# A depthwise convolution on three engines: ScalarE and GpSimd take the shared sum, VectorE keeps its running sum in PSUM

## The chip, the core and the metric

One core of a Trainium2 chip runs the whole kernel as one program. The metric is the time of an execution in device microseconds; each kernel is run several times and the median counts. Five engines matter here: TensorE (matmuls), VectorE, ScalarE and GpSimd (arithmetic on tiles of 128 partitions), and SyncE, which issues the transfers. On-chip data lie in SBUF, the results of matmuls in the eight banks of PSUM, each 128 x 512 float32.

## The reference

The reference is a small decoder trunk on 1024 tokens with 1024 features: layer 0 mixes tokens by a convolution, layer 1 by an attention with forget gates; each layer then attends to 256 memory tokens and runs a feed-forward network. Only the convolution is touched:

```python
def conformer_conv(h, w_pw1, b_pw1, w_dw, b_dw, ln_g, ln_b, w_pw2, b_pw2):
    u = h @ w_pw1 + b_pw1
    a, gate = jnp.split(u, 2, axis=-1)
    u = a * jax.nn.sigmoid(gate)
    u = lax.conv_general_dilated(          # depthwise: 31 taps, causal, each feature by itself
        u, w_dw[:, None, :], window_strides=(1,), padding=[(30, 0)],
        feature_group_count=D_MODEL) + b_dw
    u = jax.nn.silu(layernorm(u, ln_g, ln_b))
    return u @ w_pw2 + b_pw2
```

## The kernel before, in words

Features lie on the partitions, in eight chunks of 128 (called channels below, m = 0 to 7), tokens along the free dimension. `conv_layer` (L293) goes over the channels in this way:

- `gated_unit` (L362) runs for each half of the tokens. Two groups of 24 matmuls (8 chunks of the input, 3 passes each for float32 accuracy) make the gate and the value. Each group fills one PSUM bank of a pool of two (`pm`). ScalarE turns the gate into a sigmoid `sg` (L368); VectorE adds the bias to the value, multiplies by `sg` and writes `u` (L370). This copy frees the value's bank. `u` holds even and odd tokens apart, with 15 zeros ahead of each for the padding, which GpSimd sets (L301).
- `convolve` (L386) makes 512 even and 512 odd output tokens from `u`. Two neighbouring taps are treated together: the sum of both weights times the odd input is the same for even and odd outputs. This shared sum is `both`: one product with bias (L396) and 15 products added in a chain (L400). Then each half adds its own taps on the differences `d0` and `d1` of neighbouring inputs (L393, L394): 16 steps for the first half, 15 for the second (L408), each a multiplication by a per-partition weight and an addition. All of this is VectorE's. The two halves sum into their own tiles of `X`.
- After each channel VectorE adds the new `X` to `acc` of its half (L354), which is the sum that the layer norm needs.
- `memory_matrices` (L433), a generator that is advanced a step at a time from `conv_layer`, prepares matrices for the attention to the memory tokens: for each of 2 layers and 4 heads, 32 matmuls with `mem`, 16 with `kt` and 8 with `vt`. They use a PSUM pool of their own (`pps`, four banks), and ScalarE moves most of their results out (L468, L483, L501). They do not depend on the convolution and can stand between its matmuls.
- When all channels are done, `layer_norm` (L306) runs for each half (mean, L314; variance, L183; scaling, L317; SiLU on ScalarE, L318; split into high and low parts, L148), and the second linear layer (`linear`, with `add_x`, L321) follows with 16 groups of 24 matmuls.

The order of the work on each engine is fixed when the program is built: a scheduler places the instructions by their priority in the program and by its own estimate of when each could start, and each engine then runs its own list in that order. An instruction that waits holds up everything behind it on its engine. Scratch tiles called "t" in the pool `nrm` rotate through four buffers; an instruction that writes the next one waits until the last reader of that buffer is done.

The weights of a channel are split into a high part by ScalarE (`wh`, L151) and a low part by VectorE (`wl`, L148).

Of the kernel before, what the change touches and what calls it, by code (L numbers as in the profile page):

```python
# [12 lines left out]
F32 = mybir.dt.float32  # L13
F32R = mybir.dt.float32r
AF = mybir.ActivationFunctionType
ALU = mybir.AluOpType
# [3 lines left out]
P = 128  # L20
# [3 lines left out]
HALF = 512  # L24
# [12 lines left out]
HALVES = (slice(0, HALF), slice(HALF, S))  # L37
# [49 lines left out]
def trunk(ctx, tc, a, out):  # L87
    nc = tc.nc
    act, dve, pool, pe = nc.scalar, nc.vector, nc.gpsimd, nc.tensor
# [14 lines left out]
    def col(name, i):  # L104
        return par[:, COLS[name] + i : COLS[name] + i + 1]
# [22 lines left out]
    def open_x():  # L128
        xp = xpool.enter_context(tc.tile_pool(name="x", bufs=1, side="right", reuse_waits="tile"))
        return Halves(xp)  # L130

    def load_x(x, src, sl):
        for c in range(NCH):
            nc.sync.dma_start(x[:, c, sl], src[:, c, sl])

    X = open_x()
    nrm = ctx.enter_context(tc.tile_pool(name="nrm", bufs=2))
# [3 lines left out]
    def bank(p):  # L141
        return p.tile([P, HALF], F32, name="mm", tag="mm")

    def banks(n):
        return tc.tile_pool(name="pm", bufs=n, space=PSUM, reuse_waits="tile")
# [144 lines left out]
        dve.tensor_tensor(X[:, m, sl], t, X[:, m, sl], op=ALU.add)  # L290


    def conv_layer(pm, prep):  # L293
        with tc.tile_pool(name="conv", bufs=2) as cp:
            for sl in HALVES:
                next(prep)
                load_x(X, a["xT"], sl)
            def padded():

                u = cp.tile([P, 2, (PAD + S) // 2], F32, name="u")  # L300
                pool.memset(u[:, :, : PAD // 2], 0.0)  # L301
                return u

            pairs = tap_sums(cp)

            def layer_norm(s, acc):  # L306

                nm = nrm.tile([P, 4], F32, name="nm")
                with tc.high_priority(offset=SMALL_FIRST):
                    dve.tensor_scalar(nm, token_mean(acc), -1.0, None, op0=ALU.mult)  # L310
                nmb = spread(nm)
                C = [X[:, m, HALVES[s]] for m in range(NCH)]
                for c in C:
                    dve.tensor_tensor(c, c, nmb, op=ALU.add)  # L314
                rb = spread(inverse_rms(C, LN_EPS))
                for m, c in enumerate(C):
                    dve.tensor_tensor(c, c, rb, op=ALU.mult)  # L317
                    act.activation(c, c, AF.Silu, bias=col("ln_b", m), scale=col("ln_g", m))  # L318
                    split(*(y.rearrange("p (n s) -> p s n", s=2)[:, s, :] for y in ss[m]), c)

            def add_x(m, sl, t):  # L321
                x = nrm.tile([P, HALF], F32, name="x", tag="t", bufs=4)
                nc.sync.dma_start(x, a["xT"][:, m, sl])
                dve.scalar_tensor_tensor(
                    X[:, m, sl], t, col("pw2_b", m), x, op0=ALU.add, op1=ALU.add
                )

            def gate_weights(m):
                return [weights(a["pw1"][2 * m + j]) for j in (1, 0)]

            hs = operands()
            ahead = gate_weights(0)
            u = padded()
            for sl in HALVES:
                normalize(hs, "mix0", sl)
                next(prep)
                gated_unit(pm, cp, 0, ahead, hs, u[:, :, PAD // 2 :], sl)
            acc = [cp.tile([P, HALF], F32, name=f"acc{s}", bufs=1) for s in range(2)]
            for m in range(NCH):
                if m:  # L340
                    u = padded()
                    for sl in HALVES:
                        gated_unit(pm, cp, m, ahead, hs, u[:, :, PAD // 2 :], sl)
                if m + 1 < NCH:
                    ahead = gate_weights(m + 1)
                for _ in range(2):
                    next(prep, None)

                convolve(cp, m, u, pairs[:, m])
                for s, sl in enumerate(HALVES):  # L350
                    if m == 0:
                        act.copy(acc[s], X[:, m, sl])
                    else:
                        dve.tensor_tensor(acc[s], acc[s], X[:, m, sl], op=ALU.add)  # L354
            ss = operands()
            for s in range(2):
                layer_norm(s, acc[s])
            for _ in prep:
                pass
            linear(pm, lambda m: weights(a["pw2"][m]), NCH, ss, add_x)  # L360
# [15 lines left out]
    def tap_sums(cp):  # L376

        n = TAPS // 2
        w = par[:, COLS["dw_w"] : COLS["dw_w"] + NCH * TAPS].rearrange("p (m t) -> p m t", m=NCH)
        sums = cp.tile([P, NCH, n + 1], F32, name="sums", bufs=1)  # L380
        dve.tensor_copy(sums[:, :, n : n + 1], w[:, :, 2 * n :])
        two = w[:, :, : 2 * n].rearrange("p m (t s) -> p m t s", s=2)
        dve.tensor_tensor(sums[:, :, :n], two[:, :, :, 0], two[:, :, :, 1], op=ALU.add)
        return sums

    def convolve(cp, m, u, sums):  # L386


        n, k = S // 2, TAPS // 2
        even, odd = u[:, 0, :], u[:, 1, :]  # L390
        d0 = cp.tile([P, n + k], F32, name="d0")
        d1 = cp.tile([P, n + k - 1], F32, name="d1")
        dve.tensor_tensor(d0, even[:, : n + k], odd[:, : n + k], op=ALU.subtract)  # L393
        dve.tensor_tensor(d1, even[:, 1 : n + k], odd[:, : n + k - 1], op=ALU.subtract)  # L394
        both = cp.tile([P, n], F32, name="both")
        dve.tensor_scalar(  # L396
            both, odd[:, :n], sums[:, 0:1], col("dw_b", m), op0=ALU.mult, op1=ALU.add
        )
        for j in range(1, k + 1):
            dve.scalar_tensor_tensor(  # L400
                both, odd[:, j : j + n], sums[:, j : j + 1], both, op0=ALU.mult, op1=ALU.add
            )
        out = [X[:, m, sl] for sl in HALVES]
        for s, d, taps in ((0, d0, k + 1), (1, d1, k)):
            y = both
            for j in range(taps):
                w = col("dw_w", m * TAPS + 2 * j + s)
                dve.scalar_tensor_tensor(  # L408
                    out[s], d[:, j : j + n], w, y, op0=ALU.mult, op1=ALU.add
                )  # L410
                y = out[s]

# [13 lines left out]
    @contextmanager  # L428
    def prep_pools(n):
        with tc.tile_pool(name="prep", bufs=2) as pp, tc.tile_pool(name="pps", bufs=n, space=PSUM) as pq:  # L430
            yield pp, pq
# [928 lines left out]
            od[head // 2, i * HD : (i + 1) * HD, (b - 1) * P : (b + 1) * P], ol  # L1360
        )

    with prep_pools(4) as pools, banks(2) as pm:
        conv_layer(pm, chain(*(memory_matrices(*pools, l) for l in range(2))))
    sums = mem_attention(0)
    xd = dram.tile([P, NCH, S], F32, name="xd")
    first_normalized, first_weights = [], []
# [3 lines left out]
    for sl in HALVES:  # L1371
        rb = firsts if sl.start == 0 else spread(rms_of_sums(seconds, RMS_EPS))
        for c in range(NCH):
            y = X[:, c, sl]
# [71 lines left out]
```

## Time and profile before

| | |
|---|---|
| median of 3 runs | 2822.2 us (2816.68 to 2823.24) |
| profiled execution | 2825.31 us |
| its span | 2823.3 us |
| TensorE's mean granted clock in it | 0.991 |
| first write of `both` | 79.1 us |
| last step of L408 starts | 387.0 us |

Busy time is the time in which an engine had an instruction at work. Matmuls are pipelined and their ends are modelled, so two neighbouring rows of TensorE overlap in part; how often they start is read from the difference of two start times. A row of the timeline gives start, duration, engine, line and operation, with a count where equal neighbours are merged; in brackets stands how long the engine sat idle before it and who released it. A row of a group gives the count, then the summed busy time and the mean of one in nanoseconds, then idle time. The chain of waits is followed back from the last instruction and shows at each moment what the end of the program waited for.

### The profile page before, as it was taken

The numbers are of one execution on the slowest core, as the hardware profiler recorded it, in microseconds if no ns is written. First come the engines' busy times: TensorE is split into PE (matmuls) and PEld (weight loads), VectorE is DVE, ScalarE is ACT, GpSimd is POOL, SyncE is SP. The second block draws the span as 40 slices with busy tenths as digits, with TensorE's granted clock in tenths as the row PEclk, the third lists the DMA queues.
The fourth block names the chain that finished last, engine by engine and source line by source line (L and its number), as shares of the span: only waits on it lengthen the run. The fifth ranks groups of instructions, "written<-read, shape, count | busy, mean of one in ns | idle before, by whom it ended". The sixth has DMA issues, their size and how long they took to land.

```text
span 2823.3 us, 36214 instructions
## 1 busy us (share of the span) xinstructions
PE 2740.8 (97%) x12968; PEld 2261.3 (80%) x12968; DVE 2030.9 (72%) x3358; ACT 1278.3 (45%) x2293; POOL 703.1 (25%) x473
## 2 busy tenths in 40 slices
PE   8999999999999999999899999989999999989998
PEld 6777777888888877888688888878888788878886
DVE  5999984555776576777788888875546855577776
ACT  5212143433555553333466666673423655543332
POOL 0000000000065625774000000000000365525773
PEclk9999999999999999999899999999999999999999
DMA  6334364322165585652222221243213455655651
GB/s 219 120 119 135 114 206 124 101 90 70 65 230 177 178 309 187 227 199 89 69 68 70 57 65 55 69 136 98 94 64 105 149 176 190 218 208 197 227 201 61
DMA packets 165428, 390.68 MB, mean 138 GB/s; under 512 B 17264, under 2 KB 46192, under 8 KB 164992
## 3 DMA queue, kind: packets, MB, share of 16 engines
q1 hardware_dynamic: 165248, 388.37, 40.9%
q8 instruction: 102, 1.67, 0.2%
q14 instruction: 78, 0.64, 0.1%
HBM read 270.79 MB, written 113.31 MB: 136 GB/s over the span
## 4 chain that ended last, share of the span: by engine, by line
PE 74%; DVE 12%; ACT 5%; DMA 5%; issue 3%; POOL 1%; SPq 0%; DVEq 0%; POOLq 0%; ACTq 0%
PE mm L1070 34%; PE mm L269 29%; PE mm L1255 5%; DVE w L148 2%; DVE op L148 2%; DVE x L408 1%; PE mm L1341 1%; DVE x L1310 1%; DMA ua<-x 1%; ACT x L1315 1%; PE mm L1353 1%; PE mm L1354 1%; DVE both L400 1%; DVE wl L148 1%; ACT pth L151 1%
## 5 line engine op out<-in xcount | busy, mean ns | idle before, releaser
L1070 PE MATMUL mm<-op,w 128*128 128x512 f32 x5424 | 1242.4, 391 | 24.5 <-ACT m L955 8.7
L1070 PEld LDWEIGHTS mm<-op,w 128*128 128x128 f32 x5424 | 1020.5, 189 | 243.2 <-ACT m L955 9.6
L269 PE MATMUL mm<-op,wh 128*128 128x512 f32 x1056 | 330.5, 394 | 4.2 <-DVE op L148 4.2
L148 DVE TENSOR_TENSOR w<-r,w 128x512 fp32r<-128x512 f32 x264 | 262.6, 998 | 30.5 <-ACT w L653 30.5
L653 ACT CAST w<-r 128x512 fp32r<-128x512 f32 x264 | 163.3, 622 | 262.0 <-PE mm L1070 233.2
L269 PEld LDWEIGHTS mm<-op,wh 128*128 128x128 f32 x1056 | 200.2, 190 | 48.5 <-DVE op L148 6.5
L1255 PE MATMUL mm<-op,wh 128*128 128x512 f32 x736 | 231.4, 396 | 0.0
L148 DVE TENSOR_TENSOR w<-t,w 128x512 fp32r<-128x512 f32 x180 | 178.2, 1005 | 63.2 <-ACT w L653 63.1
L269 PE MATMUL mm<-op,wl 128*128 128x512 f32 x528 | 210.5, 400 | 7.1 <-DVE wl L148 6.2
L207 POOL TENSOR_TENSOR r<-v,mhalf 128x4 f32<-128x4 f32 (+1 forms) x15 | 16.8, 1117 | 741.0 <-DVE v L205 741.0
L647 POOL TENSOR_TENSOR t<-r,t 128x512 f32<-128x512 f32 x104 | 174.9, 1681 | 91.4 <-DVE w L148 54.2
L653 ACT CAST w<-t 128x512 fp32r<-128x512 f32 x180 | 112.0, 622 | 169.8 <-PE mm L1070 140.6
L151 ACT CAST wh<-raw 128x1024 fp32r<-128x1024 f32 x96 | 100.7, 1050 | 193.8 <-PE mm L269 97.5
L865 POOL TENSOR_TENSOR x<-x,x 128x512 f32<-128x512 f32 x112 | 160.2, 1455 | 112.6 <-ACT x L878 101.6
L967 DVE TENSOR_TENSOR x<-mm,x 128x512 f32<-128x512 f32 x160 | 109.5, 684 | 91.1 <-PE mm L1070 73.7
L1255 PEld LDWEIGHTS mm<-op,wh 128*128 128x128 f32 x736 | 139.2, 189 | 26.7
L269 PE MATMUL mm<-op,xsh 128*128 128x512 f32 x512 | 158.0, 393 | 0.0
L1255 PE MATMUL mm<-op,wl 128*128 128x512 f32 x368 | 155.0, 421 | 1.9 <-ACT q L1275 1.9
L151 ACT CAST pth<-mm 128x512 fp32r<-128x512 f32 (+1 forms) x224 | 105.9, 495 | 108.5 <-PE mm L556 80.8
L408 DVE SCALAR_TENSOR_TENSOR x<-d,par,x 128x512 f32<-128x512 f32 x232 | 154.5, 746 | 0.0
L647 POOL TENSOR_TENSOR t<-r,r 128x512 f32<-128x512 f32 x52 | 80.2, 1542 | 295.1 <-DMA r<-in_ff_w 191.0
L1315 ACT ACTIVATE x<-x,nb 128x128 f32<-128x128 f32 (+7 forms) x128 | 99.5, 778 | 109.3 <-DVE nb L1313 100.0
(188 smaller groups left out, 4689.6 us busy)
## 6 DMA issues: line engine op xcount, KB each, us to landing
r<-in_ff_w SPq DMA_DIRECT2D x128, 512.0 KB, 4.0
op<-ua SPq DMA_DIRECT2D x80, 512.0 KB, 6.8
us<-x SPq DMA_DIRECT2D x128, 256.0 KB, 2.9
op<-us SPq DMA_DIRECT2D x64, 512.0 KB, 5.6
raw<-mvo SPq DMA_DIRECT2D x32, 512.0 KB, 3.4
ua<-ul SPq DMA_DIRECT2D x64, 256.0 KB, 2.2
ua<-uh SPq DMA_DIRECT2D x60, 256.0 KB, 2.3
raw<-in_pw SPq DMA_DIRECT2D x24, 512.0 KB, 4.7
```

Of the source, the lines that this page charges most:

```text
L148: dve.tensor_tensor(lo, src, hi.bitcast(F32), op=ALU.subtract)
L151: act.copy(hi, src)
L269: pe.matmul(out_ps, x, y, start=i == 0, stop=i == len(terms) - 1)
L400: dve.scalar_tensor_tensor(both, odd[:, j : j + n], sums[:, j : j + 1], both, op0=ALU.mult, op1=ALU.add)
L408: dve.scalar_tensor_tensor(out[s], d[:, j : j + n], w, y, op0=ALU.mult, op1=ALU.add)
L647: (dve if g in (2, 3, UP, UP + 1) else pool).tensor_tensor(t, raws[g, x], raws[g, y], op=ALU.subtract)
L653: act.copy(highs[n][0], raws[steps[n][:2]])
L865: eng.tensor_tensor(u[g, x], y1, y2, op=op_)
L967: dve.tensor_tensor(v, sums[key], v, op=ALU.add)
L1070: pe.matmul(sums[key], y, z, start=first and i == 0, stop=n == last_of[key] and i == len(terms) - 1, skip_group_check=True,)
L1255: pe.matmul(t, x, y, start=n == 0, stop=n == len(terms) - 1)
L1315: act.activation(x[:, :n], x[:, :n], AF.Exp, bias=nb, accum_out=rs)
```

## The change

- The product with bias that starts `both` becomes a ScalarE activation. Each of the 15 further products becomes a ScalarE activation with a scale, written to a scratch tile `tap` (one of the four "t" buffers), and a GpSimd addition `both = both + tap`.
- The steps on `d0` and `d1` stay on VectorE, but the running sum is kept in a PSUM bank `acc` of a new pool with one bank; only the last step of each half writes `X`. Both halves use the same bank, so the second half's chain follows the first's.
- The pool for the memory matrices' products shrinks from four banks to three, which makes room for the new bank.
- `d0` and `d1` have one buffer each instead of two.

```diff
-    def convolve(cp, m, u, sums):
+    def convolve(cp, pc, m, u, sums):
         n, k = S // 2, TAPS // 2
         even, odd = u[:, 0, :], u[:, 1, :]
-        d0 = cp.tile([P, n + k], F32, name="d0")
-        d1 = cp.tile([P, n + k - 1], F32, name="d1")
+        both = cp.tile([P, n], F32, name="both")
+        act.activation(both, odd[:, :n], AF.Identity, scale=sums[:, 0:1], bias=col("dw_b", m))
+        for j in range(1, k + 1):
+            t = nrm.tile([P, HALF], F32, name="tap", tag="t", bufs=4)
+            act.activation(t, odd[:, j : j + n], AF.Copy, scale=sums[:, j : j + 1])
+            pool.tensor_tensor(both, both, t, op=ALU.add)
+        d0 = cp.tile([P, n + k], F32, name="d0", bufs=1)
+        d1 = cp.tile([P, n + k - 1], F32, name="d1", bufs=1)
         dve.tensor_tensor(d0, even[:, : n + k], odd[:, : n + k], op=ALU.subtract)
         dve.tensor_tensor(d1, even[:, 1 : n + k], odd[:, : n + k - 1], op=ALU.subtract)
-        both = cp.tile([P, n], F32, name="both")
-        dve.tensor_scalar(
-            both, odd[:, :n], sums[:, 0:1], col("dw_b", m), op0=ALU.mult, op1=ALU.add
-        )
-        for j in range(1, k + 1):
-            dve.scalar_tensor_tensor(
-                both, odd[:, j : j + n], sums[:, j : j + 1], both, op0=ALU.mult, op1=ALU.add
-            )
-        out = [X[:, m, sl] for sl in HALVES]
+        acc = bank(pc)
         for s, d, taps in ((0, d0, k + 1), (1, d1, k)):
             y = both
             for j in range(taps):
+                o = X[:, m, HALVES[s]] if j == taps - 1 else acc
                 w = col("dw_w", m * TAPS + 2 * j + s)
-                dve.scalar_tensor_tensor(
-                    out[s], d[:, j : j + n], w, y, op0=ALU.mult, op1=ALU.add
-                )
-                y = out[s]
+                dve.scalar_tensor_tensor(o, d[:, j : j + n], w, y, op0=ALU.mult, op1=ALU.add)
+                y = acc
...
-    with prep_pools(4) as pools, banks(2) as pm:
-        conv_layer(pm, chain(*(memory_matrices(*pools, l) for l in range(2))))
+    with prep_pools(3) as pools, banks(2) as pm, banks(1) as pc:
+        conv_layer(pm, pc, chain(*(memory_matrices(*pools, l) for l in range(2))))
```

The scheduler's order changes with it. VectorE before, at channel 1 (`x_79` and `x_80` are the tiles of `X` of its two halves, `d_866` and `d_867` its differences):

```order
L393 TENSOR_TENSOR d_866<-u 128x527
L394 TENSOR_TENSOR d_867<-u 128x526
L396 TENSOR_SCALAR both<-u,sums,par 128x512
L400 SCALAR_TENSOR_TENSOR both<-u,sums,both 128x512 x15
L408 SCALAR_TENSOR_TENSOR x_79<-d_866,par,both 128x512
L408 SCALAR_TENSOR_TENSOR x_80<-d_867,par,both 128x512
L408 SCALAR_TENSOR_TENSOR x_79<-d_866,par,x_79 128x512
```

VectorE now, at the same channel (`mm` on the left of L409 is the new bank; the `u` of L370 is channel 2's):

```order
L402 TENSOR_TENSOR d_948<-u 128x526
L409 SCALAR_TENSOR_TENSOR mm<-d_947,par,both 128x512
L409 SCALAR_TENSOR_TENSOR mm<-d_947,par,mm 128x512 x11
L370 SCALAR_TENSOR_TENSOR u<-mm,par,sg 128x2x256
L409 SCALAR_TENSOR_TENSOR mm<-d_947,par,mm 128x512 x3
L409 SCALAR_TENSOR_TENSOR x_79<-d_947,par,mm 128x512
L409 SCALAR_TENSOR_TENSOR mm<-d_948,par,both 128x512
L354 TENSOR_TENSOR acc_567<-acc_567,x_79 128x512
```

The two halves' chains no longer alternate, and the copy of the next channel's `u` stands behind steps that need `both`.

ScalarE before, from channel 2's sigmoids to channel 3's (`vt` is a memory product):

```order
L368 ACTIVATE sg<-mm,par 128x512 x2
L151 CAST wh<-raw 128x1024 x2
L468 COPY vt<-mm 128x512
L368 ACTIVATE sg<-mm,par 128x512 x2
L151 CAST wh<-raw 128x1024
```

ScalarE now, at the same place:

```order
L368 ACTIVATE sg<-mm,par 128x512 x2
L151 CAST wh<-raw 128x1024 x2
L394 ACTIVATE both<-u,par,sums 128x512
L397 ACTIVATE tap<-u,sums 128x512 x15
L467 COPY vt<-mm 128x512
L368 ACTIVATE sg<-mm,par 128x512 x2
L151 CAST wh<-raw 128x1024 x2
```

The taps stand ahead of the next channel's sigmoids.

TensorE before, in the second linear layer after the layer norm (`op` with `wh` and `wl` are its matmuls, `praw,vt` memory products):

```order
L269 MATMUL mm<-op,wl 128x512 x2
L269 MATMUL mm<-op,wh 128x512 x3
L269 MATMUL mm<-praw,vt 128x512 x4
L269 MATMUL mm<-op,wh 128x512
L269 MATMUL mm<-op,wl 128x512
```

TensorE now, at the same place:

```order
L269 MATMUL mm<-op,wl 128x512 x2
L269 MATMUL mm<-op,wh 128x512 x2
L269 MATMUL mm<-praw,vt 128x512 x4
L269 MATMUL mm<-mem,praw 128x256 x32
L269 MATMUL mm<-kt,praw 128x256 x12
L269 MATMUL mm<-praw,vt 128x512 x2
```

One more head of the memory matrices stands inside the second linear layer.

More of the change, by code (lines that the diff above doesn't have):

```diff
@@ L290, in add_to_x, with conv_layer @@
         dve.tensor_tensor(X[:, m, sl], t, X[:, m, sl], op=ALU.add)
-    def conv_layer(pm, prep):
+    def conv_layer(pm, pc, prep):
         with tc.tile_pool(name="conv", bufs=2) as cp:
@@ L347, in conv_layer @@
                     next(prep, None)
-                convolve(cp, m, u, pairs[:, m])
+                convolve(cp, pc, m, u, pairs[:, m])
                 for s, sl in enumerate(HALVES):
```

## The prediction

> **What bounds the kernel now.** I read the page's first two lines, then busy time by window for the convolution (the change touches nothing else), then its timeline and its chain of waits.
>
> ```profile
> span 2823.3 us, 36214 instructions
> PE 2740.8 (97%) x12968; PEld 2261.3 (80%) x12968; DVE 2030.9 (72%) x3358; ACT 1278.3 (45%) x2293; POOL 703.1 (25%) x473
> ```
>
> The profiled execution took 2825.3 us, 2.0 more than its span; the median of the three runs is 2822.2. The sum below is a shift of this execution, and I add it to the median. TensorE is at work 97% of the span, so only its waits can be won. Two moments cut out the stretch: VectorE completes `u` of channel 0 at 76.7 (the first row's start plus its duration) and of channel 7 at 350.3; the last operand of the layer norm is written at 442.55.
>
> ```profile
> 75.94 0.75 DVE L370 SCALAR_TENSOR_TENSOR u<-mm,par,sg 128x512 f32<-128x512 f32 x1 [2.56 <-PE mm L269]
> 349.52 0.74 DVE L370 SCALAR_TENSOR_TENSOR u<-mm,par,sg 128x512 f32<-128x512 f32 x1
> 441.25 1.30 DVE L148 TENSOR_TENSOR op<-x,op 128x512 fp32r<-128x512 f32 x2 [1.20 <-ACT op L151]
> ...
> core 0: us, PE busy (x) PEld busy (x) DVE busy (x) ACT busy (x) POOL busy (x), PEclk, DMA share, GB/s
> 76.70:350.30 273.60, 269.94 (x1145) 214.48 (x1144) 268.70 (x387) 55.44 (x91) 0.75 (x6) 1.00 0.38 121
> 350.30:442.60 92.30, 90.53 (x402) 69.84 (x401) 78.52 (x122) 47.22 (x84) 2.01 (x2) 1.00 0.61 195
> ```
>
> In the windows, each engine's busy us follows the length. Seven channels take 273.6, 39.1 each. VectorE is full (268.7), but so is TensorE (269.9): the memory-matrix products fill what the gated units leave. TensorE's idle time is 3.7 + 1.8 = 5.4 us in both windows together. That caps what a lighter VectorE can give while the matmuls stay the same. The chain there passes from VectorE to TensorE and back:
>
> ```profile
> 286.75 0.76 DVE both L400
> 288.33 14.00 DVE x L408 x21
> 302.93 6.62 DVE x L408 x10
> 312.61 25.13 PE mm L269 x108
> ```
>
> **The change part by part.** *Off VectorE:* per channel 15 additions to `both` and the first product.
>
> ```profile
> 121.86 7.84 DVE L400 SCALAR_TENSOR_TENSOR both<-u,sums,both 128x512 f32<-128x512 f32 x10
> 131.72 10.68 DVE L408 SCALAR_TENSOR_TENSOR x<-d,par,x 128x512 f32<-128x512 f32 x16
> L396 DVE TENSOR_SCALAR both<-u,sums,par 128x512 f32<-128x512 f32 x8 | 4.3, 543 | 0.0
> ```
>
> Ten of L400, where each reads what the one before wrote, take 7.84: (7.84 − 0.75)/9 = 0.788 from start to start. Sixteen of L408, where two chains alternate, take (10.68 − 0.75)/15 = 0.662. So 15 × 0.788 + 0.54 = 12.4 us leave per channel. But both halves now run through one bank, one chain after the other, so each step waits for the step before: 31 × (0.788 − 0.662) = 3.9 come back. Net 8.5 less per channel, 68 in all, worth at most the 5.4 above.
>
> *The step in PSUM.* No VectorE instruction of before writes PSUM. The lower bound is 0.662 (waiting for the step before costs nothing). The upper one goes by ScalarE, whose scaled 128x512 pass takes 62 ns more with PSUM on one side than a pass in SBUF: 0.85.
>
> ```profile
> L501 ACT ACTIVATE o<-mm,mem_r 128x512 f32<-128x512 f32 x32 | 21.8, 686 | 51.8 <-DMA mqk<-o 25.0 <-DMA mvo<-o 20.3 <-PE mm L269 5.9
> L182 ACT ACTIVATE t<-x 128x512 f32<-128x512 f32 x32 | 18.8, 624 | 8.2 <-DVE x L324 4.3 <-DVE acc L183 3.8
> L370 DVE SCALAR_TENSOR_TENSOR u<-mm,par,sg 128x512 f32<-128x512 f32 x16 | 11.6, 747 | 2.9 <-PE mm L269 2.9
> L408 DVE SCALAR_TENSOR_TENSOR x<-d,par,x 128x512 f32<-128x512 f32 x232 | 154.5, 746 | 0.0
> ```
>
> I take 0.788, since the same operation reads PSUM in 747 and SBUF in 746 ns. The Trainium skill (VectorE: DVE Perf Modes, section The TRN2 errata) gives VectorE 120 fixed cycles from PSUM and 58 from SBUF at 0.96 GHz; as an estimate from that page, 0.065 us on each of 195 steps, 12.6 us more. The two rows above do not show that difference for reads; no row shows a write.
>
> *Onto ScalarE and GpSimd:* per channel one scaled pass with bias, 15 scaled passes, 15 additions in a row.
>
> ```profile
> L865 POOL TENSOR_TENSOR x<-x,x x112: 1282/1305/1821, 771.9 to 2459.5; 128x512 f32<-128x512 f32 x112
> L951 POOL TENSOR_TENSOR x<-x,m x72: 1288/1740/2308, 1117.1 to 2777.9; 128x512 f32<-128x512 f32 x72
> 789.38 1.45 POOL L647 TENSOR_TENSOR t<-r,r 128x512 f32<-128x512 f32 x1 [0.25 <-issue]
> 790.91 1.62 POOL L647 TENSOR_TENSOR t<-r,t 128x512 f32<-128x512 f32 x1
> L967 DVE TENSOR_TENSOR x<-mm,x x160: 674/682/693, 1060.0 to 2807.5; 128x512 f32<-128x512 f32 x160
> L148 DVE TENSOR_TENSOR w<-r,w x264: 675/689/1820, 714.9 to 2787.6; 128x512 fp32r<-128x512 f32 x132
> L148 DVE TENSOR_TENSOR wl<-raw,wh 128x1024 fp32r<-128x1024 f32 x24 | 28.7, 1220 | 12.5 <-ACT wh L151 12.1 <-DMA x<-in_xT 0.4
> ```
>
> The triples are shortest, median, longest in ns. An addition on GpSimd takes 1.30; one that needs the result of the one before starts 0.08 after its end (789.38 + 1.45 to 790.91). So 15 take 15 × 1.38 = 20.7. VectorE's operations with one input in PSUM (L967) never stretch in the feed-forward stages, where GpSimd adds; those with both in SBUF reach 1820, and GpSimd's reach 2308. So the PSUM steps go untouched, but four operations per channel with both inputs in SBUF (one `wl`, d0, d1, `acc`) fall under the additions; each makes one about 0.44 longer (1.74 against 1.30): 1.8. The lead, first pass, first tap and two hand-overs, is about 1.5 (two passes of 0.62 to 0.69). **From `u` to `both`: 24 us**, where VectorE took 12.4. ScalarE's 0.7 per tap stays ahead of GpSimd's 1.38; four buffers let it run four taps ahead, no more.
>
> *Is that beside other work?* By the order it isn't. VectorE has the copy of the next channel's `u` behind steps that wait for `both`: from `both` to the completed next `u` stand 28, 23, 27, 23, 28, 23, 27 steps, 179 over seven channels, 25.6 each. TensorE's fourth group of the next gated unit needs the bank which the first of these two copies frees, and the next taps need the second. So per channel, one after the other: 24 + 25.6 × 0.788 (20.2) + one `wl` and one `acc` (1.8) + two copies (1.3) − 0.5 (four steps follow another instruction and start at 0.662) = 46.8. Seven are 328, against 273.6: **+54**.
>
> TensorE's group of 24 matmuls needs 8 × 0.68 = 5.5 us (three start every 0.68):
>
> ```profile
> 97.27 0.62 PE L269 MATMUL mm<-op,wh 128*128 128x512 f32 x2
> ...
> 97.95 0.39 PE L269 MATMUL mm<-op,wh 128*128 128x512 f32 x1
> ```
>
> Between the two copies VectorE has about 11 steps and a `wl`, 10 us, so TensorE isn't late. The sigmoid queued behind the taps on ScalarE goes when the eleventh addition is done, some 19 us after `u`, before `both` at 24: no cost. In channels 1, 3 and 5 three evacuations of memory products stand before it, waiting on their stores; the cover there is about 3 us, and what runs over it is added.
>
> *The tail.* After the last `u`: 24 + 16 × 0.788 + 0.6 = 37.2 until the first half is summed. The layer norm took 53.6 from the end of both sums (388.98) to 442.55. Now 14 steps of the second half are woven into it: 53.6 + 14 × 0.662 = 62.9. Together 100.1 against 92.3: **+8**.
>
> ```profile
> 387.68 1.30 DVE L354 TENSOR_TENSOR acc<-acc,x 128x512 f32<-128x512 f32 x2
> ```
>
> *Memory products.* The last of eight heads ran before the second linear layer; now it stands in TensorE's row behind that layer's first group, after the norm. Its price, two records a matmul: 32 with `mem` 14.0; 16 with `kt` 4.53 × 32/20 = 7.2; 8 with `vt` 7.0: **+28**.
>
> ```profile
> 75.74 13.97 PE L269 MATMUL mm<-mem,praw 128*128 128x256 f32 x64
> 112.45 4.53 PE L269 MATMUL mm<-kt,praw 128*128 128x256 f32 x20
> 57.98 7.03 PE L269 MATMUL mm<-praw,vt 128*128 128x512 f32 x16
> ```
>
> The third PSUM bank fewer for these products, single d0 and d1, and the loads moved with them on SP's queue I cost at nothing: TensorE now idles some 11 us per channel (46.8 less its work of four groups, 22, and half a head, 14), which covers their waits; without that cover they would cost a few us per head.
>
> Sum: 54 + 8 + 28 = **+90**, 2915 for the profiled execution, **2912** for the median. Bounds: additions at 1.29 back to back and undisturbed (19.4 a channel), −26; all at 1.74 + 0.08 (27.3), +38; steps at 0.662, −25; at 0.85, +12. That is 2861 to 2962.
>
> **The rivals.**
> *Not slower (0.05): GpSimd's chain hides.* It decides where a channel is back at 39.1: with steps at 0.788, additions at 0.9; with 0.662, at 1.1. The shortest addition is 1.28, which speaks against it; VectorE's 8.5 us for each channel speak for it. It gives at best the 5.4 of idle time: 2817.
> *The clock (0.13).* TensorE had no long wait in the convolution; now it has one in each channel. Where it last waited, its granted clock was 0.68:
>
> ```profile
> 40.00:50.00 10.00, 7.83 (x30) 6.19 (x29) 2.28 (x6) 2.31 (x5) 1.01 (x1) 0.68 0.52 162
> ```
>
> At 0.68 a group takes 8.1 and stays under VectorE's 10. At half clock it takes 11, and a late sigmoid adds to it: about 3.5 a channel, 7 × 3.5 = 25, 2937. The Trainium skill (TensorE: Matmul & The Clock Gate, Part 1) has the clock halve after an idle window of about 3.4 us and return after as much work; the row agrees that waits lower it, and with it only 3.4 us of each burst, a loss of 1.7 per wait, would be slow.
> *Every addition is stretched (0.10):* the PSUM steps collide with GpSimd after all; +38, 2950. L967 speaks against it.
> *Steps cheap and the last head hidden (0.08):* 0.662, and the head fits under the norm: 90 − 25 − 28 = +37, 2859.
>
> **How the numbers follow.** My forecast has 0.64. What a measurement of this kernel can tell from no change is about 0.3%, 8.5 us; only the first rival comes near, and I split its 0.05 into 0.03 within and 0.02 faster by more (the order could hide more than I see). The range 2866 to 2951 holds the forecast, the clock and most of the third rival, and most of the way to both bounds.
>
> **What would show it.** Right: `u` copies (L370) some 47 us apart per channel; VectorE idle before the first step of a channel, waiting for GpSimd's additions; additions 1.4 to 1.5 apart; steps 0.79 apart; channel 7's `u` near 404; matmuls with `mem` amid the second linear layer. Wrong: additions under 1.1 or steps under 0.7; `u` copies 39 apart; VectorE idle on TensorE instead of GpSimd.

## The result, and the profile after

The changed kernel takes 2913.7 us (median of 4 runs, 2907.1 to 2914.5) against 2822.3 for the kernel before (2816.7 to 2823.2): a ratio of 1.0323, 95% interval 1.0303 to 1.0343. It is 91 us slower. The prediction said 2912, with a range of 2866 to 2951.

The head of the page of the changed kernel:

```profile
span 2911.4 us, 36417 instructions
PE 2765.4 (95%) x12968; PEld 2270.9 (78%) x12968; DVE 1968.0 (68%) x3230; ACT 1361.8 (47%) x2421; POOL 862.0 (30%) x593
```

VectorE is 63 us less busy than before (1968.0 against 2030.9), and the span is 88 us longer. TensorE has the same 12968 matmuls and falls from 97% to 95%. It is busy 24.6 us longer (2765.4 against 2740.8), at a mean granted clock of 0.981 against 0.991; the other 63 us of the longer span are waits. Where they lie is shown by the windows of the convolution, of the layer norm and from there to the first result of the second linear layer:

```profile
core 0: us, PE busy (x) PEld busy (x) DVE busy (x) ACT busy (x) POOL busy (x), PEclk, DMA share, GB/s
76.10:397.60 321.50, 267.03 (x1074) 208.20 (x1073) 212.20 (x272) 122.25 (x191) 141.38 (x111) 0.92 0.28 92
397.60:501.70 104.10, 88.85 (x360) 64.70 (x359) 71.39 (x109) 57.92 (x101) 22.20 (x17) 0.95 0.51 159
501.70:534.60 32.90, 32.90 (x129) 23.87 (x129) 1.44 (x2) 8.50 (x16) 0.00 (x0) 1.00 0.61 183
```

In the convolution no engine is full any more: TensorE, busy for 270 of 273.6 us before, is busy for 267 of 321.5, VectorE for 212 and GpSimd for 141. When nobody is full and the stretch is longer, look for work that stands in a row. VectorE's timeline over channel 0, from the copy that completes its `u` to the copy that completes the next channel's:

```profile
75.39 0.75 DVE L370 SCALAR_TENSOR_TENSOR u<-mm,par,sg 128x512 f32<-128x512 f32 x1 [2.55 <-PE mm L269]
...
98.58 0.76 DVE L409 SCALAR_TENSOR_TENSOR mm<-d,par,both 128x512 f32<-128x512 f32 x1 [15.60 <-POOL both L398]
99.38 11.05 DVE L409 SCALAR_TENSOR_TENSOR mm<-d,par,mm 128x512 f32<-128x512 f32 x14
110.46 0.75 DVE L409 SCALAR_TENSOR_TENSOR x<-d,par,mm 128x512 f32<-128x512 f32 x1
111.25 0.76 DVE L409 SCALAR_TENSOR_TENSOR mm<-d,par,both 128x512 f32<-128x512 f32 x1
111.91 0.75 DVE L370 SCALAR_TENSOR_TENSOR u<-mm,par,sg 128x512 f32<-128x512 f32 x1
112.58 6.29 DVE L409 SCALAR_TENSOR_TENSOR mm<-d,par,mm 128x512 f32<-128x512 f32 x8
...
119.91 2.33 DVE L409 SCALAR_TENSOR_TENSOR mm<-d,par,mm 128x512 f32<-128x512 f32 x3
122.15 0.74 DVE L370 SCALAR_TENSOR_TENSOR u<-mm,par,sg 128x512 f32<-128x512 f32 x1
```

`u` is complete at 76.14; the first step that reads `both` starts 22.4 later, after an idle time that GpSimd ends; 28 steps and the next channel's `u` follow, complete at 122.89. Neither of that channel's two copies waited for TensorE. The waits from the first `u` to channel 7's first step show the same for all eight channels (engine, line and releaser; total, times, longest):

```profile
DVE mm L409 <- POOL both L398: 116.0, 8, 17.4
...
PE mm L269 <- DVE u L370: 41.3, 5, 11.8
```

VectorE waits for GpSimd in each of the eight channels, and TensorE five times for VectorE's copy: the chain that was forecast. A channel of the kernel before can be cut at the same two moments, the completed `u` and the first steps that read `both`; here channel 3 on VectorE:

```profile
192.18 1.41 DVE L370 SCALAR_TENSOR_TENSOR u<-mm,par,sg 128x512 f32<-128x512 f32 x2
...
209.40 1.41 DVE L408 SCALAR_TENSOR_TENSOR x<-d,par,both 128x512 f32<-128x512 f32 x2
...
231.75 1.41 DVE L370 SCALAR_TENSOR_TENSOR u<-mm,par,sg 128x512 f32<-128x512 f32 x2
```

From `u` (193.59) to `both` it was 15.8, and from there to the next `u` (233.16) 23.8; the means of the seven channels are 16.2 and 22.9. Now they are 23.0 and 22.9. The second leg is as long as before, with fewer but slower steps in it, and the whole loss of the loop lies in the first: 7 × 6.8 = 48.

The durations of the changed kernel's additions and steps (shortest, median, longest in ns):

```profile
L398 POOL TENSOR_TENSOR both<-both,tap x120: 1261/1285/1780, 77.8 to 420.0; 128x512 f32<-128x512 f32 x120
...
L409 DVE SCALAR_TENSOR_TENSOR mm<-d,par,mm x216: 742/756/757, 99.4 to 453.3; 128x512 f32<-128x512 f32 x108
```

The last memory head stands ahead of the second linear layer's results. TensorE's timeline, then VectorE's with the first and the last of these results:

```profile
504.95 13.98 PE L269 MATMUL mm<-mem,praw 128*128 128x256 f32 x64
518.77 5.36 PE L269 MATMUL mm<-kt,praw 128*128 128x256 f32 x24
...
500.37 1.29 DVE L148 TENSOR_TENSOR op<-x,op 128x512 fp32r<-128x512 f32 x2 [1.21 <-ACT op L151]
...
533.82 0.75 DVE L324 SCALAR_TENSOR_TENSOR x<-mm,par,x 128x512 f32<-128x512 f32 x1 [21.07 <-PE mm L269]
...
612.71 0.75 DVE L324 SCALAR_TENSOR_TENSOR x<-mm,par,x 128x512 f32<-128x512 f32 x1
```

The same two results before:

```profile
446.93 0.75 DVE L324 SCALAR_TENSOR_TENSOR x<-mm,par,x 128x512 f32<-128x512 f32 x1 [4.38 <-PE mm L269]
...
525.55 0.75 DVE L324 SCALAR_TENSOR_TENSOR x<-mm,par,x 128x512 f32<-128x512 f32 x1
```

With these moments the difference can be laid out (us):

| stretch | before | after | difference |
|---|---|---|---|
| to `u` of channel 0 | 76.7 | 76.1 | -0.6 |
| seven channels, `u` to `u` | 273.6 | 321.5 | +47.9 |
| last `u` to last norm operand | 92.3 | 104.1 | +11.8 |
| from there to the first result of linear layer 2 | 5.1 | 32.9 | +27.8 |
| first to last result | 78.6 | 78.9 | +0.3 |
| the rest of the program | 2297.0 | 2297.9 | +0.9 |

### The profile page after: what moved, and what is told of

It is laid out like the page before. It is cut to its first block, busy times and chain, and to the rows that moved or that the text cites. A ratio compares the mean times of both kernels' runs of the same rounds, so it can differ in the third digit from the quotient of the medians.

```text
span 2911.4 us, 36417 instructions
## 1 busy us (share of the span) xinstructions
PE 2765.4 (95%) x12968; PEld 2270.9 (78%) x12968; DVE 1968.0 (68%) x3230; ACT 1361.8 (47%) x2421; POOL 862.0 (30%) x593
## 3 DMA queue, kind: packets, MB, share of 16 engines
HBM read 270.79 MB, written 113.31 MB: 132 GB/s over the span
## 4 chain that ended last, share of the span: by engine, by line
PE 66%; DVE 15%; POOL 6%; ACT 5%; DMA 4%; issue 4%; SPq 0%; POOLq 0%; DVEq 0%; ACTq 0%
PE mm L1069 33%; PE mm L269 21%; POOL both L398 5%; PE mm L1254 5%; DVE mm L409 4%; DVE op L148 2%; DVE w L148 2%; PE mm L1340 1%; DVE x L1309 1%; ACT x L1314 1%; PE mm L1352 1%; PE mm L1353 1%; DVE x L966 1%; DVE wl L148 1%; DVE ptl L148 1%
## 5 line engine op out<-in xcount | busy, mean ns | idle before, releaser
L269 PE MATMUL mm<-op,wh 128*128 128x512 f32 x1056 | 339.4, 403 | 4.7 <-DVE op L148 4.7
L269 PE MATMUL mm<-op,wl 128*128 128x512 f32 x528 | 216.0, 410 | 47.9 <-DVE u L370 41.3
L1254 PE MATMUL mm<-op,wh 128*128 128x512 f32 x736 | 230.3, 394 | 0.0
L398 POOL TENSOR_TENSOR both<-both,tap 128x512 f32<-128x512 f32 x120 | 161.2, 1343 | 211.3 <-ACT tap L397 202.5
L409 DVE SCALAR_TENSOR_TENSOR mm<-d,par,mm 128x512 f32<-128x512 f32 x216 | 162.9, 754 | 5.8
L646 POOL TENSOR_TENSOR t<-r,r 128x512 f32<-128x512 f32 x52 | 78.9, 1516 | 290.3 <-DMA r<-in_ff_w 248.3
L269 PEld LDWEIGHTS mm<-op,wl 128*128 128x128 f32 x528 | 102.9, 195 | 75.4 <-DVE u L370 43.4
```

What stands on the lines that cost most here:

```text
L269: pe.matmul(out_ps, x, y, start=i == 0, stop=i == len(terms) - 1)
L398: pool.tensor_tensor(both, both, t, op=ALU.add)
L409: dve.scalar_tensor_tensor(o, d[:, j : j + n], w, y, op0=ALU.mult, op1=ALU.add)
L646: (dve if g in (2, 3, UP, UP + 1) else pool).tensor_tensor(t, raws[g, x], raws[g, y], op=ALU.subtract)
L1254: pe.matmul(t, x, y, start=n == 0, stop=n == len(terms) - 1)
```

## The experiments

The theory is that of the prediction: GpSimd's chain of additions and VectorE's steps stand in a row, because VectorE has the copy of the next `u` behind steps that need `both`; a displaced memory head comes on top. Rivals are the running sum in a single PSUM bank (and the bank that the memory products lost to it), additions that slow VectorE, and waits of TensorE. A difference between kernels is taken from their ratios to the kernel before, with 2820 us to 1; between stretches from the traces, since the part behind the linear layer varied by 18 us (2286 to 2304) among profiles, and the part ahead of the first `u` by 4 (72.4 to 76.7), whatever the change.

### One part alone

**The PSUM sum without the other engines.** The changed kernel with `both` on VectorE again:

```diff
-            act.activation(t, odd[:, j : j + n], AF.Copy, scale=sums[:, j : j + 1])
-            pool.tensor_tensor(both, both, t, op=ALU.add)
+            dve.scalar_tensor_tensor(
+                both, odd[:, j : j + n], sums[:, j : j + 1], both, op0=ALU.mult, op1=ALU.add
+            )
```

> The changed kernel with the shared sum back on VectorE; the PSUM running sum, its one bank and the third prep bank stay. Theory (the series of GpSimd's chain and VectorE's steps is the cost, with the displaced memory head): nothing waits for GpSimd, all heads stand ahead of the second linear layer, and what is left is the dependent step of 0.788 against 0.662, at most 31 x 0.126 x 7 = 27 us and less where the scheduler puts a shared-sum step between two of them: 2830 to 2851, nearest 2835. Rival (the running sum in one PSUM bank, and one bank fewer for the memory products, is the cost): about 2914, as the changed kernel.

Measured: 2837.0 us, ratio 1.0059 (1.0038 to 1.0080), 17 us more than before. The theory's 2835 holds; the PSUM bank is not where 91 us went. VectorE's timeline in this kernel shows why it is so cheap; here a step of the shared sum in SBUF and a step in the PSUM bank take turns:

```profile
199.46 0.75 DVE L398 SCALAR_TENSOR_TENSOR both<-u,sums,both 128x512 f32<-128x512 f32 x1
200.13 0.75 DVE L411 SCALAR_TENSOR_TENSOR mm<-d,par,mm 128x512 f32<-128x512 f32 x1
200.78 0.75 DVE L398 SCALAR_TENSOR_TENSOR both<-u,sums,both 128x512 f32<-128x512 f32 x1
```

Each starts 0.66 after the one before, as two chains in SBUF did. What a step loses in a single chain (0.79) is lost to the wait for the step before, not to PSUM. The order differs from the changed kernel's in more than that: the copies of `u` run ahead of the steps, so that the seven channels take 253.0 us, 20.5 less than before, and the steps left over make the stretch from the last `u` to the last norm operand 122.1, 29.8 more.

**The other engines without the PSUM sum.** The kernel before, with only the shared sum given away:

```diff
-        dve.tensor_scalar(
-            both, odd[:, :n], sums[:, 0:1], col("dw_b", m), op0=ALU.mult, op1=ALU.add
-        )
+        act.activation(both, odd[:, :n], AF.Identity, scale=sums[:, 0:1], bias=col("dw_b", m))
...
+            act.activation(t, odd[:, j : j + n], AF.Copy, scale=sums[:, j : j + 1])
+            pool.tensor_tensor(both, both, t, op=ALU.add)
```

> The kernel before with only the shared sum moved to ScalarE and GpSimd; both running sums stay in X in SBUF, four prep banks, d0 and d1 double. Theory (series): per channel 24 for the shared sum, then all 31 steps at 0.662 (20.5), since in its order the copies of u stand behind all of them, two acc and two copies (2.6): 47 us, 7 x (47 - 39.1) = 55, tail up to 12, the displaced head 28 (its order has it): 2900 to 2920. Rival (the PSUM sum is the cost): about 2822.

Measured: 2911.6 us, ratio 1.0322 (1.0296 to 1.0347): the whole loss, without any PSUM sum, and with four banks for the memory products and two buffers each for `d0` and `d1` as before. Channel 0 on VectorE:

```profile
96.24 1.41 DVE L406 SCALAR_TENSOR_TENSOR x<-d,par,both 128x512 f32<-128x512 f32 x2 [15.59 <-POOL both L400]
97.58 19.29 DVE L406 SCALAR_TENSOR_TENSOR x<-d,par,x 128x512 f32<-128x512 f32 x29
...
118.58 0.74 DVE L370 SCALAR_TENSOR_TENSOR u<-mm,par,sg 128x512 f32<-128x512 f32 x1
```

The steps alternate and are fast, (19.29 - 0.75)/28 = 0.662, but all 31 stand ahead of the second copy: 119.3 less 73.8, the end of the copy before, is 45.5. The six channels behind it took 46.9 each.

### The length of the chain

**Eight taps.** The changed kernel with a shorter sum; it leaves out seven of the 15 products, so its result is not the convolution:

```diff
-        for j in range(1, k + 1):
+        for j in range(1, 9):
             t = nrm.tile([P, HALF], F32, name="tap", tag="t", bufs=4)
```

> The changed kernel with 8 of the 15 additions of the shared sum: taps 9 to 15 of that sum are left out of the computation. Theory (series): the path from u to the shared sum is 7 x 1.35 = 9.5 us shorter, so a channel falls from 45.9 to 36.5, and no further, since TensorE needs 36 for its four groups and half a head: 7 x 9.4 = 66 less, and 9.5 less in the tail if TensorE lets it; the displaced head stays: 2838 to 2850. Rival (GpSimd's chain is hidden, the loop is held by VectorE's steps or by TensorE at its lower clock): no more than 10 us less, 2904 to 2914.

Measured: ratio 1.0152 (1.0125 to 1.0179), 2863.5 us, some 48 less than the change. The rival (no more than 10) is out, the theory's number (64 to 76) is missed by 16 to 28. A channel took 40.4, not 36.5. Its timeline:

```profile
153.08 0.75 DVE L370 SCALAR_TENSOR_TENSOR u<-mm,par,sg 128x512 f32<-128x512 f32 x1
...
167.26 0.76 DVE L409 SCALAR_TENSOR_TENSOR mm<-d,par,both 128x512 f32<-128x512 f32 x1 [5.98 <-POOL both L398]
168.06 11.05 DVE L409 SCALAR_TENSOR_TENSOR mm<-d,par,mm 128x512 f32<-128x512 f32 x14
...
194.40 0.75 DVE L370 SCALAR_TENSOR_TENSOR u<-mm,par,sg 128x512 f32<-128x512 f32 x1
```

From `u` to `both` it is 13.4 (153.83 to 167.26); the mean of seven channels is 13.3 against 23.0, so the 9.7 us did go. But from `both` to the next `u` it is 27.9 here, 27.1 on average, against 22.9. The scheduler, which lays the order out anew for each program, put 30 or 31 steps ahead of the second copy where the changed kernel has 25.6: five steps of 0.79 are 3.9 of the 4.2. The series is confirmed; what I missed is that an edit of one chain also moves the copy.

### The series itself

**Steps held back.** Nothing is made faster; VectorE's steps of a channel are merely tied behind the copies of the next channel's `u`:

```diff
+                    copies.append(nc.cur_bb.bb.instructions[-1].name)
+                    finish_channel(*held, copies)
...
-                convolve(cp, pc, m, u, pairs[:, m])
+                held = m, u, convolve(cp, pc, m, u, pairs[:, m])
...
+                if j == 0 and copies:
+                    tc.add_manual_dep(
+                        nc.cur_bb.bb.instructions[-1], copies[s],
```

> The changed kernel with VectorE's steps of a channel put behind the two copies of the next channel's u (the first half's behind the first copy, the second half's behind the second), nothing else. Theory (what costs is that GpSimd's chain and VectorE's steps stand in series, not the work itself): the additions of one channel now run beside the steps of the channel before, and a channel takes what TensorE needs, 36 to 38 instead of 45.9: 7 x 8 to 10 = 56 to 69 less; the tail of 104 and the displaced head of 28 stay: 2845 to 2860. Rival (GpSimd's additions slow VectorE's steps when they do run beside them, PSUM or not, by some 0.44 each): 20 of 31 steps stretched, VectorE at 42 to 44 a channel: 2885 to 2900.

Measured: 2848.2 us, ratio 1.0110 (1.0085 to 1.0136): 60 us less than the change, inside the theory's range. Seven channels take 263 us, and TensorE is busy for 254 of them. That additions now run beside steps is seen on GpSimd and VectorE:

```profile
149.92 22.32 POOL L406 TENSOR_TENSOR both<-both,tap 128x512 f32<-128x512 f32 x15 [16.54 <-ACT tap L405]
...
157.86 8.66 DVE L422 SCALAR_TENSOR_TENSOR mm<-d,par,mm 128x512 f32<-128x512 f32 x11
```

Eleven steps in 8.66 are (8.66 - 0.75)/10 = 0.79 apart, exactly as without additions beside them, and fifteen additions take 22.3 against 20.7 to 21.6. The 47 additions that had only steps with an input in PSUM beside them took 1.26 to 1.30 us, no more than those with nothing beside them; each that took over 1.35 had an operation with both inputs in SBUF beside it. The rival is out.

**The same with heads ahead.** In the held-back kernel the memory products are emitted before the last steps and the norm:

```diff
+            for _ in prep:
+                pass
             finish_channel(*held)
             ss = operands()
             for s in range(2):
                 layer_norm(s, acc[s])
-            for _ in prep:
-                pass
```

> The kernel of the held-back steps with the memory products emitted ahead of the last channel's steps and the norm, so that no head stands in the second linear layer. Theory: the head's 28 us fill TensorE's idle time in the tail, except some 10 to 15, for TensorE has 84 us of heads and 14 of rest in a tail of 104: 15 to 28 less than with the held-back steps alone, 2818 to 2840, about the time before and at best 5 us less, since TensorE was busy for all but 5 us of this stretch before. Rival (the last head costs nothing where it stood, the linear layer waits for its operands anyway): no change against the held-back steps alone.

Measured: 2841.5 us, ratio 1.0074 (1.0056 to 1.0093), 10 us less than with the held-back steps alone: the theory's direction, short of its 15 to 28. Of the 106.6 us from the last `u` to the last norm operand TensorE is still idle for 8.6, which the head does not fill. Its timeline after the last `u`, and one of ScalarE's evacuations:

```profile
346.51 1.13 PE L269 MATMUL mm<-kt,praw 128*128 128x256 f32 x4 [1.73 <-ACT o L501]
...
358.20 1.99 PE L269 MATMUL mm<-mem,praw 128*128 128x256 f32 x8 [0.72 <-ACT o L519]
...
359.71 0.69 ACT L519 ACTIVATE o<-mm,mem_r 128x512 f32<-128x512 f32 x1 [1.56 <-DMA mvo<-o]
```

The products of a head wait for the evacuation of products before them, and some evacuations for the store of the tile `o` that they are to write. TensorE's waits for evacuations are 6.8 us of that idle time.

**The sum in SBUF.** The last kernel, but every step writes `X`:

```diff
-                o = X[:, m, HALVES[s]] if j == taps - 1 else acc
+                o = X[:, m, HALVES[s]]
```

> The kernel with held-back steps and heads ahead, but with the running sums in X in SBUF in place of the PSUM bank. Theory (a VectorE operation with both inputs in SBUF and a GpSimd addition take turns, one with an input in PSUM doesn't): steps beside additions take 1.3 to 1.8 in place of 0.75 and additions as much, some 17 of 31 steps a channel, VectorE at 40 to 44 a channel against TensorE's 36 to 38: 25 to 45 us more than with the PSUM bank. Rival (the PSUM bank buys nothing here): within 6 us of the kernel with it, or less by the alternating steps.

Measured: 2892.0 us, ratio 1.0253 (1.0232 to 1.0274): 50 more than with the bank, the theory's direction and somewhat above its 45. The steps, the additions, and the window of the seven channels:

```profile
L421 DVE SCALAR_TENSOR_TENSOR x<-d,par,x x232: 742/752/1778, 98.8 to 426.7; 128x512 f32<-128x512 f32 x116
...
L406 POOL TENSOR_TENSOR both<-both,tap x120: 1271/1602/2152, 75.0 to 400.9; 128x512 f32<-128x512 f32 x120
...
73.30:374.70 301.40, 267.28 (x1083) 208.94 (x1081) 274.35 (x257) 123.57 (x192) 169.08 (x111) 0.95 0.30 98
```

Of 232 steps 85 take over a microsecond, up to 1778 ns, where those with an input in PSUM never passed 766, and the median addition grows from 1289 to 1602. So the PSUM bank does buy something, but in an order in which steps and additions overlap; in the order of the changed kernel they hardly do.

### The displaced head and its stores

**One head more in the loop** of the changed kernel:

```diff
-                for _ in range(2):
+                for _ in range(3 if 2 <= m <= 5 else 2):
                     next(prep, None)
```

> The changed kernel with three instead of two steps of the memory products emitted in channels 2 to 5, so that one head more lies in the convolution and the last no longer in the second linear layer. Theory: TensorE idles 9 us a channel there and takes the 28 us for nothing: 2914 - 28 = 2886, and linear layer 2 without TensorE idle or VectorE waits of 10 and 21 us. Rival (TensorE's groups, slowed by the lower granted clock, are on the path of each u, so more work in the loop costs what it saves): 2905 to 2925.

Measured: 2900.1 us, ratio 1.0283 (1.0259 to 1.0306), 11 less. Both theories missed: the gain is there, and most of it is given back. From the last `u` to the first result of the linear layer it is 107.6 instead of 137.0, 29 less, and that result waits only 4.40 us for TensorE. But the seven channels take 339.7, 18 more. The given-back time is not TensorE's: no copy of `u` in those channels waited for it. In this order, all 31 steps of four channels stand ahead of the second copy, as with eight taps, and those channels take 50.1 to 50.9.

**The head in the tail**, with the loop's order untouched:

```diff
+            for _ in prep:
+                pass
             ss = operands()
             for s in range(2):
                 layer_norm(s, acc[s])
-            for _ in prep:
-                pass
```

> The changed kernel with the last memory head emitted ahead of the norm in place of behind it; the convolution's order is untouched on VectorE and TensorE. Theory (the head's 28 us are TensorE's work without cover, so they cost what TensorE has no idle time for): TensorE was idle for 15 of the 104 us from the last u to the last norm operand, and the head takes that: 2914 - 15 = 2899. Rival (in the linear layer the head only stood in front of something that was late anyway): 2910 to 2914.

Measured: 2907.2 us, ratio 1.0311 (1.0286 to 1.0337): 3 less than the change, which the intervals cannot tell from nothing; the traces have 5 less from the last `u` to the last result of the linear layer. The expected 15 did not come. TensorE is still idle for some 14 us of the tail, and 8 of them are waits of the heads' own products for evacuations:

```profile
404.57 1.12 PE L269 MATMUL mm<-praw,vt 128*128 128x512 f32 x2 [3.36 <-ACT o L482]
...
414.20 3.07 PE L269 MATMUL mm<-mem,praw 128*128 128x256 f32 x13 [1.89 <-ACT o L500]
```

**Four buffers for the products on their way out**, tried on three kernels: held back with heads ahead, the kernel before, and the changed kernel.

```diff
-                    o = pp.tile([P, 4, P], F32, name="o")
+                    o = pp.tile([P, 4, P], F32, name="o", bufs=4)
```

> The kernel of held-back steps and heads ahead, with four buffers in place of two for the memory products on their way out (tile o). Theory: what it still lacks against the kernel before is TensorE's idle time behind the evacuations of these products, which stand between the taps on ScalarE and wait for their stores (4.5 us in each channel that has them, some 12 in all): 2842 - 8 to 12 = 2830 to 2834, and the channels of 40 go to 36 to 37. Rival (the wait is ScalarE's queue of taps alone, not the stores): unchanged, 2838 to 2845.

> The kernel before with four buffers in place of two for the memory products on their way out, nothing else: does the gain of these buffers belong to the held-back kernel alone? Theory (in the kernel before TensorE is busy for all but 5 us of the 366 from the first u to the last norm operand, so there is no wait for a store to remove): 2814 to 2819, no difference that can be told. Rival (the buffers help any order): 2819 - 18 = 2801.

> The changed kernel with four buffers in place of two for the memory products on their way out, nothing else. Theory (in the convolution GpSimd's chain and VectorE's steps are the path and hide TensorE's waits for these evacuations; only in the tail and the linear layer are they uncovered): u copies 45 to 46 us apart as before the edit, and 5 to 15 us less behind them: 2899 to 2909. Rival (the third PSUM bank fewer and these stores are a good part of what the change costs): 2885 to 2896.

Measured, held back: 2823.6 us, ratio 1.0012 (0.9997 to 1.0026), 18 less, more than the theory's 8 to 12, and level with the kernel before. Before: 2821.2, ratio 0.9998 (0.9984 to 1.0013), no difference. Changed: 2892.3, ratio 1.0274 (1.0247 to 1.0300), 14 less by the ratio and 21 by the medians, so that theory (5 to 15) and rival (18 to 29) cannot be told apart by the time. In the held-back kernel TensorE's waits for the evacuations are gone. Its timeline about the last `u`, and the windows of the loop and of the stretch from there to the first result of the linear layer (columns as in the windows above):

```profile
323.71 7.20 PE L269 MATMUL mm<-kt,praw 128*128 128x256 f32 x32
330.75 7.23 PE L269 MATMUL mm<-praw,vt 128*128 128x512 f32 x16
...
74.00:325.10 251.10, 250.54 (x1076) 201.62 (x1075) 208.37 (x256) 121.64 (x192) 145.88 (x111) 1.00 0.35 118
325.10:441.60 116.50, 110.40 (x469) 82.14 (x468) 86.09 (x127) 65.60 (x116) 22.79 (x17) 1.00 0.62 199
```

TensorE is at work for 250.5 of 251.1 us in the loop, so a VectorE with still less to do would gain nothing there. Part of the heads' work has moved behind the loop: from the first `u` to the last result of the linear layer this kernel takes 450.3, the kernel before 449.6, which cannot be told from no change.

For the changed kernel I had the loop untouched. It was not: 44.7 a channel against 45.9, 9 us. Again the order moved: from `both` to the next `u` it is 21.6 on average against 22.9, while `u` to `both` stayed at 23.0. Behind the last `u`, up to the last result of the linear layer, the traces have only 1.4 less: TensorE's waits for these evacuations are gone there too, but it waits 6.7 us for the evacuation of `vt` instead of 1.1. The rest is no more than profiles differ by ahead of the first `u` and behind the linear layer.

## Why the prediction was right

**The path.** The step that carried the number was "one after the other": chain, steps, copies. The two half-changes show it from both sides (17 us without the chain on other engines, 91 with it alone), and tying the steps behind the copies took 60 of the 91 away without making any instruction faster.

**The number.** That 2912 came within 2 us is in part luck. The loop was forecast 6 us too high and the tail 4 too low, and the profiled execution of before lay 3 us above its median: the traces differ by 88, the medians by 91. The lower bound is 1 us off in its own terms (22.5 less 19.4, eight times, is 25 and not 26), which changes nothing.

**From `u` to `both`: 24.** Measured 23.0 on average over seven channels, 23.7 for the last. The additions came 1.38 apart as forecast at the start (15 in 20.7) and took up to 21.6 where operations of VectorE with both inputs in SBUF fell beside them; I had given these 1.8; they took up to 0.9, on average 0.5. The lead was 1.8 where I had 1.5. Together this is the error of the loop: 7 × 1.0 = 7, less 1 for the other leg, where 54 were forecast and 47.9 measured.

**From `both` to the next `u`: 22.8.** Measured 22.9.

**The step in PSUM: 0.788.** Measured (11.05 - 0.76)/13 = 0.79. The bounds 0.662 and 0.85 were needed in the range only. By the estimate from the Trainium skill (VectorE: DVE Perf Modes, section The TRN2 errata) each step would have been 0.065 longer; no run here shows that: 756 ns with PSUM on both sides stand against 746 in SBUF before (L408), and the starts are the same 0.79 apart.

**The tail: +8.** Measured +11.8. The first half was summed 38.2 after the last `u` (37.2 forecast), and the norm behind it took 65.9 (62.9). Part of the 3 us is the clock that I had kept out of this place. TensorE's eight small matmuls for the mean of the first half, now and then before:

```profile
435.86 1.87 PE L158 MATMUL mm<-mean_col,acc 128*128 128x1 f32 x8 [4.04 <-DVE acc L354]
...
389.03 1.05 PE L158 MATMUL mm<-mean_col,acc 128*128 128x1 f32 x8 [0.57 <-DVE acc L354]
```

The spread of the mean behind them took 1.92 instead of 1.05; together this is 1.7. The granted clock was 0.50 in both places now, and 1.00 before.

**The head: +28.** Measured +27.8, by its own rows. But the sentence that the third PSUM bank and the products' waits cost nothing because TensorE's idle time covers them holds in the loop only. In the tail these waits make idle time that a head did not use, so that moving the head there gave 3 to 5 us and not 15. What the third bank costs by itself was not run; with four banks and the shared sum given away the loss was the same 91.

**The rivals.** GpSimd's chain did not hide, and its shortest addition, 1261 ns, is above the 0.9 to 1.1 at which it would have. The additions were not stretched by PSUM steps. The clock did fall, and TensorE's timeline behind a wait shows by how much:

```profile
112.72 0.79 PE L269 MATMUL mm<-op,wl 128*128 128x512 f32 x1 [7.22 <-DVE u L370]
113.31 1.05 PE L269 MATMUL mm<-op,wh 128*128 128x512 f32 x2
...
114.59 1.05 PE L269 MATMUL mm<-op,wh 128*128 128x512 f32 x2
...
118.07 0.63 PE L269 MATMUL mm<-op,wh 128*128 128x512 f32 x2
...
118.76 0.63 PE L269 MATMUL mm<-op,wh 128*128 128x512 f32 x2
```

After 7.22 us of waiting, three matmuls take 1.28 (113.31 to 114.59), later 0.69 (118.07 to 118.76). The granted clock is 0.50 from 112.7 to 117.6 and 1.00 from 117.7 on. The Trainium skill (TensorE: Matmul & The Clock Gate, Part 1) has the clock return after at least one busy window of about 3.4 us; the trace agrees, with 4.9 us here and 3.4 to 5.8 behind the three other waits of over 7 us (9.5, 11.7 and 11.8). The granted clock in the loop's window is 0.92 against 1.00 before. It cost the loop next to nothing: one copy waited 0.51 us for TensorE, the last one, and the second copy of each other channel came 9.4 to 10.7 us behind the first without waiting. The cover that the prediction named held, by little.

## What to carry to other kernels

Work taken off a busy engine helps only where nothing else is full beside it: here TensorE left 5 us in the stretch, and the best order found for the changed kernel comes out level with the old one. A longer latency on another engine is paid in every round when the list of the engine that waits for it has the next round's input behind the wait (here 23.0 us in place of 16.2, seven times); tying the consumer one round later took most of it away. Where a scheduler orders the program anew after every edit, compare its orders before costing an edit, and after an experiment check that it moved only what it was to move.

## What the hardware showed that I had not expected

- A step of VectorE with PSUM on both sides costs what one in SBUF costs, to 10 ns in duration (756 against 746) and the same in starts (0.66 when two chains alternate, 0.79 in a single chain).
- The collision of VectorE and GpSimd goes by the operands and in both directions: with both inputs in SBUF, steps of 0.75 reach 1.78 and additions of 1.29 become 1.60; with one input in PSUM the steps stay at 0.79 apart beside fifteen additions in a row.
- A wait of 4 us was enough to nearly double the time of TensorE's next small matmuls (1.87 for 1.05), and waits of 7 to 12 us were followed by 3.4 to 5.8 us at half the granted clock.
- Idle time that a stage makes for itself (products waiting for their own evacuations and stores) need not take in more work of the same kind: a head of 28 us put into a tail with 15 us of idle time saved 3 to 5. Four buffers for the stores removed these waits in the held-back order; in the tail of the changed kernel others took their place.
